# Two mixture-of-experts layers on one core: the first expert's products by halves around the gather, the last experts' sums around the up product, and the norm rows in the last down product

## Chip, core and metric

The kernel runs on one NeuronCore of a Trainium2 chip. The metric is the device time of one execution in microseconds (us), and the figure compared is the median of several executions. One execution was also recorded by the hardware profiler; its rows are what everything below is read from.

## What is computed

A trunk of two layers over 512 latent tokens (and 256 context tokens in layer 0) of width 1024. Each layer has a mixer (attention and pooling, then a short convolution) and after it a mixture of experts, which is where the change lies. Every one of 16 experts picks the 64 tokens with the highest affinity, so that the tokens of an expert are gathered, passed through three products with the expert's own weights, and summed back into the tokens' rows:

```python
def _expert_choice_ffn(u, w_router, w_g, w_u, w_d):
    b, n, _ = u.shape
    cap = CAPACITY_FACTOR * n // N_EXPERTS          # 64 of 512
    logits = jnp.einsum('bnd,de->ben', u, w_router, preferred_element_type=jnp.float32)
    aff = jax.nn.softmax(logits, axis=1)
    gate, idx = lax.top_k(aff, cap)
    bidx = jnp.arange(b)[:, None, None]
    xe = u[bidx, idx]
    hg = jnp.einsum('becd,edf->becf', xe, w_g)
    hu = jnp.einsum('becd,edf->becf', xe, w_u)
    ye = jnp.einsum('becf,efd->becd', jax.nn.silu(hg) * hu, w_d) * gate[..., None].astype(u.dtype)
    return jnp.zeros_like(u).at[bidx, idx].add(ye)

# in reference(), per layer:
h_lat = _post_norm(h_lat, m_lat[5] * f_lat, ln_ffn_g[layer], ln_ffn_b[layer])
```

Every weight of the three products is read once per execution: 16 experts x 3 matrices x 1024 x 1024 x 4 bytes are 201 MB in each layer, and 490 MB are moved in all.

## The kernel before

**Blocks and queue.** The weights pass through ten buffers of 2 MB, the blocks (names `blk`, numbered). Each of an expert's three matrices (`g`, `u`, `d`) is two blocks, one for each half of the contraction. `self.queue` lists all loads in the order in which they are used. A load is issued on the sync engine's queue (SP) at the point where a product has finished with a block: `next_load(b)` (L216 is its DMA) puts the next item of the queue into block `b` as one transfer of 2 MB; `next_half(b, h)` (L239) does the same in two transfers of 1 MB, the first as soon as half of the block has been read. With ten blocks, the block that a product frees is filled with weights used five products later. The last expert's `u` and `d` come in four pieces of 512 KB per block. SP issues in program order, so a transfer that waits for its block holds up those behind it.

**An expert.** `moe` runs over the experts in order. For expert `e`: `product("g", ...)` (16 rows of matmuls per half, L1341), `Silu` on ScalarE, `product("u", ...)`, `hid = silu(g) * u` on VectorE (L1401), four transposes of it (`p_t`, L1409) with a copy (`hT`, L1411), `scatter_sel` (one matmul `p_sb`, L1351, and a compare that gives the scatter matrix `st`), and `product("d", ...)`, whose result is scaled and split by `split_y`. The result of expert `e` is summed into the rows of all tokens during expert `e + 1`: `scatters(0)` and `scatters(2)`, four matmuls each (`p_sc`, L1369) and four VectorE updates (L1372). Up to expert 14 these stand behind the `u` product, on both sides of the transposes; in expert 15 they stand between the halves of `g` and behind `g`.

**The gather.** `gather` (L1319) forms the token columns `xe` of two experts, 16 matmuls for each half of the contraction, with ScalarE copies (L1328). For experts 2 to 15 it is spread over the preceding experts; for the first it runs where it is used: one half ahead of `g`, the other as `between`, ahead of the second half of `g`. Only the products `g` and `u` of expert 0 free their blocks by `next_half`; all others use `next_load`.

**The end of a layer.** The last `d` product is `out_mm`, in two column halves, with the sums (`sum_mm`, L1457) of the first half inside the second. In layer 1 the rows of the last norm's gain and shift (`ln_row`, 16 matmuls `p_gb`, L284, and four ScalarE copies) are made in expert 14, ahead of its `d` product, in a block that is no longer needed (`self.spare`). After it come the norm and the output. At three places in the kernel matmuls on zeros (`p_idle`) are run whose results nobody reads.

Of the kernel before, what the change touches and what calls it, by code (L numbers as in the profile page):

```python
# [16 lines left out]
P = 128  # L17
D = 1024
KO = D // P
# [6 lines left out]
KH = KO // 2  # L26
KEYS = S + C
KT = KEYS // P
NE = 16
# [96 lines left out]
def _pack(inp):  # L126
# [59 lines left out]
    rows=(4, 5, 9, 10, 15, 17),  # L186
# [4 lines left out]
class Trunk:  # L191
# [1094 lines left out]
    def moe(self, layer):  # L1286
        nc, tc, ins = self.nc, self.tc, self.ins
        last = layer == 1
# [4 lines left out]
        with tc.tile_pool(name=f"ex{layer}", bufs=2) as wk:  # L1293
            side = lambda v: [v[:, 0:512], v[:, 512:1024]]
            one = lambda name: wk.tile([P, 512], F32, name=name, bufs=1)
            g0 = side(wk.tile([P, D], F32, name="gb0", tag="yp", bufs=1)), [one("st"), one("hT")]
            rows = [lambda v=v: self.ln_row(4 * layer + v, g0[v], ALPHA) for v in range(2)]
# [14 lines left out]
            def gather(g, j0, j1, e0=0, e1=2, tag="sc"):  # L1312
                n = (e1 - e0) * CAP
                if j0 % KH == 0:
                    xes[g].append(wk.tile([P, KH, 2, CAP], F32, name="xe", bufs=3))
                pg = self.bank(tag, (P, j1 - j0, n), "p_ga")
                for j in range(j0, j1):
                    for t in range(TT):
                        nc.tensor.matmul(pg[:, j - j0], H[:, t, j * P:(j + 1) * P],  # L1319
                                         sels[g][:, t, e0:e1].rearrange("p e s -> p (e s)"),  # L1320
                                         start=t == 0, stop=t == TT - 1)
                for j in range(j0, j1):
                    o = xes[g][j // KH][:, j % KH, e0:e1].rearrange("p e s -> p (e s)")
                    if e1 - e0 == 1 and j % 2:
                        nc.vector.tensor_scalar(o, pg[:, j - j0], self.FG[:, 0, j:j + 1], self.FG[:, 1, j:j + 1],
                                                ALU.mult, ALU.add)
                    else:
                        nc.scalar.activation(o, pg[:, j - j0], AF.Identity, bias=self.FG[:, 1, j:j + 1],  # L1328
                                             scale=self.FG[:, 0, j:j + 1])

            def product(tag, lhs, name, between=None, by_halves=False):
                o = self.bank(tag)
                for h in range(2):
                    if h and between:
                        between()
                    W, b = self.w[f"{name}_{h}"]
                    W = W.rearrange("p (k n) -> p k n", k=KH)
                    for kk in range(KH):
                        k = h * KH + kk
                        for hf in range(2):  # L1340
                            nc.tensor.matmul(o[64 * hf:64 * hf + 64], lhs(k), W[:, kk, hf * 512:hf * 512 + 512],  # L1341
                                             start=k == 0, stop=k == KO - 1)
                        if by_halves and kk % 2:
                            self.next_half(b, kk // 2)
                    if not by_halves:
                        self.next_load(b)
                return o

            def scatter_sel(e):
                pb = self.bank("tr", name="p_sb")  # L1350
                nc.tensor.matmul(pb, self.identb[:, e:e + 1].to_broadcast([P, P]), self.slotb, start=True, stop=True)  # L1351
                st = wk.tile([P, S], F32R, name="st", bufs=1)
                nc.vector.tensor_scalar(st, pb, self.cv("slot1"), None, ALU.is_equal)
                return st

            def split_y(p_d, yp, m5):

                n = yp.shape[2]
                ye = self.rows()[:, 0:n]
                nc.vector.tensor_tensor(ye, p_d, m5, ALU.mult)  # L1360
                for hf in range(2):
                    r, q = slice(64 * hf, 64 * hf + 64), slice(64 - 64 * hf, 128 - 64 * hf)
                    nc.scalar.copy(yp[r, hf], ye[r])  # L1363
                    nc.vector.tensor_tensor(yp[q, hf], ye[r], yp[r, hf].bitcast(F32), ALU.subtract)  # L1364

            def scatter(e, st, yp, t):
                pp = [self.bank(name="p_sc") for _ in range(2)]
                for hf in range(2):
                    nc.tensor.matmul(pp[hf], st[:, t * P:(t + 1) * P], yp[:, hf], start=True, stop=True)  # L1369
                for hf in range(2):  # L1370
                    a = A[:, t, hf * 512:hf * 512 + 512]
                    nc.vector.scalar_tensor_tensor(a, pp[hf], self.gateT[:, t, e:e + 1], a, ALU.mult, ALU.add)  # L1372
# [4 lines left out]
            for t in range(TT):  # L1377
                self.residual(t, g0)
            gather(0, 0, 4)
            prev, gb = None, []  # L1380
            for e in range(NE):
                xe = xes[e // 2]
                before = prev

                def scatters(t0):
                    for t in (t0, t0 + 1) if before else ():
                        scatter(*before, t)

                p_g = product("g", lambda k: xe[k // KH][:, k % KH, e % 2], f"g{layer}_{e}", (lambda: scatters(0) if e == NE - 1 else None) if e else lambda: gather(0, 4, KO), e == 0)
                sg = wk.tile([P, 512], F32, name="sg", bufs=1)  # L1390
                nc.scalar.activation(sg, p_g, AF.Silu)  # L1391
                if e == NE - 1:
                    scatters(2)
                g = e // 2 + 1
                if g < NE // 2 and e % 2 == 0:
                    sel_build(g)
                p_u = product("u", lambda k: xe[k // KH][:, k % KH, e % 2], f"u{layer}_{e}", None, e == 0)
                if e == 0 and self.late:
                    self.late()
                hid = self.rows()  # L1400
                nc.vector.tensor_tensor(hid, sg, p_u, ALU.mult)  # L1401

                if e < NE - 1:
                    scatters(0)
                if g < NE // 2:
                    gather(g, 4 * (e % 2), 4 * (e % 2) + 4, tag="g")
                p_t = self.bank("tr", (P, 4, P), "p_t")
                for q in range(4):
                    nc.tensor.transpose(p_t[:, q], hid[:, q * P:(q + 1) * P], self.cv("ident"))  # L1409
                hT = wk.tile([P, 4, P], F32, name="hT", bufs=1)  # L1410
                nc.vector.tensor_copy(hT, p_t)  # L1411
                if e < NE - 1:
                    scatters(2)
                st = scatter_sel(e)
                if last and self.spare and not gb:
                    gb += [self.spare[:, v * D:v * D + D] for v in range(2)]
                    g1 = [side(v) for v in gb]
                    for v in range(2):
                        self.ln_row(4 * layer + 2 + v, g1[v], 1.0)
                lhs = lambda k: hT[:, k % 4, (k // 4) * CAP:(k // 4) * CAP + CAP]  # L1420
                yp = wk.tile([P, 2, 512], F32R, name="yp", bufs=1)
                if e < NE - 1:
                    split_y(product("d", lhs, f"d{layer}_{e}"), yp, self.m5b)
                    prev = (e, st, yp)
            nc.scalar.preload_act_table_set("natural_log_exp_and_others")

# [9 lines left out]
            def out_mm(c, k0, k1):  # L1436
                W, b = self.w[f"d{layer}_{e}_{c}"]
                W = W.rearrange("p (k n) -> p k n", k=KO)
                for k in range(k0, k1):
                    for q in range(2):  # L1440
                        nc.tensor.matmul(outs[c][64 * q:64 * q + 64], lhs(k), W[:, k, q * 256:q * 256 + 256],
                                         start=k == 0, stop=k == KO - 1)
                if k1 == KO:
                    self.next_load(b)
                    split_y(outs[c], yps[:, c], m5[:, c])
# [21 lines left out]
            hs = wk.tile([P, TT, 2], F32, name="l_hs", bufs=1)  # L1467
# [34 lines left out]
                return self.rsqrt(x, v, wk)  # L1502

            out_mm(0, 0, KO)
            out_mm(1, 0, KH)
            for t in range(TT):
                if t < 2 + last:
# [8 lines left out]
            if last:  # L1516
# [42 lines left out]
                idle = self.bank(name="p_idle")  # L1559
# [196 lines left out]
```

## Time and profile before

| | |
|---|---|
| median of 3 runs | 1444.56 us (1442.07 to 1447.09) |
| the profiled execution | 1447.51 us |
| its span, first to last instruction | 1445.7 us |
| TensorE (PE) busy | 1379.2 us, 95% |
| VectorE (DVE), ScalarE (ACT), GpSimd (POOL) busy | 48%, 23%, 8% |
| moved by DMA | 490.35 MB, 339 GB/s over the span |
| mean granted TensorE clock | 0.979 |

The page cuts the span into 40 slices of 36 us. The experts of layer 0 run from about 291 to 740 us and those of layer 1 from about 971 to 1422 us; in both stretches the DMA row reads 9 in nearly every slice, at 426 or 427 GB/s, and so does the PE row. Busy PE is not PE at its peak, since ends of matmuls are modelled. PEclk is the clock granted to TensorE: 1.00 is 2.4 GHz and 0.50 is 1.2 GHz.

### The profile page before, as it was taken

The numbers are of one execution on the slowest core, as the hardware profiler recorded it, in microseconds if no ns is written. First come the engines' busy times: TensorE is split into PE (matmuls) and PEld (weight loads), VectorE is DVE, ScalarE is ACT, GpSimd is POOL, SyncE is SP. The second block draws the span as 40 slices with busy tenths as digits, with TensorE's granted clock in tenths as the row PEclk, the third lists the DMA queues.
The fourth block names the chain that finished last, engine by engine and source line by source line (L and its number), as shares of the span: only waits on it lengthen the run. The fifth ranks groups of instructions, "written<-read, shape, count | busy, mean of one in ns | idle before, by whom it ended". The sixth has DMA issues, their size and how long they took to land.

```text
span 1445.7 us, 17480 instructions
## 1 busy us (share of the span) xinstructions
PE 1379.2 (95%) x7212; PEld 766.8 (53%) x7212; DVE 690.1 (48%) x1221; ACT 333.7 (23%) x654; POOL 120.1 (8%) x151
## 2 busy tenths in 40 slices
PE   7999989899999999999979999999999999999996
PEld 4875547654444444444358787764444444444333
DVE  3574758713343343333466878761343343343245
ACT  3455661311011011011143223141111111111112
POOL 3111630050000000000020000014000000000000
PEclk9999999899999999999989999999999999999998
DMA  9347337989999999999974554659999999999991
GB/s 369 140 162 302 128 123 305 380 305 420 427 426 427 427 427 425 427 427 426 418 289 150 221 226 190 251 243 374 428 426 426 427 427 427 426 426 427 426 404 62
DMA packets 42527, 490.35 MB, mean 339 GB/s; under 512 B 4752, under 2 KB 5200, under 8 KB 13136
## 3 DMA queue, kind: packets, MB, share of 16 engines
q1 hardware_dynamic: 41856, 486.10, 81.5%
q10 hardware_dynamic: 592, 3.15, 0.6%
q8 instruction: 56, 0.92, 0.3%
q14 instruction: 23, 0.19, 0.0%
HBM read 487.13 MB, written 2.10 MB: 338 GB/s over the span
## 4 chain that ended last, share of the span: by engine, by line
PE 65%; DMA 20%; DVE 10%; ACT 2%; issue 1%; POOL 0%; DVEq 0%; SPq 0%; ACTq 0%
PE p_g L1341 11%; PE p_d L1341 10%; PE p_u L1341 10%; DMA blk<-wu 7%; DMA blk<-wg 5%; DMA blk<-wd 5%; PE p_ga_g L1319 5%; PE p_sc_sc L1369 3%; DMA blk<-wmod 2%; PE p_c_sc L253 2%; PE p_c_sc L255 2%; PE p_c_sc L254 2%; PE p_y_sc L253 2%; PE p_y_sc L255 2%; PE p_y_sc L254 1%; PE p_o L947 1%
## 5 line engine op out<-in xcount | busy, mean ns | idle before, releaser
L1341 PE MATMUL p_u<-blk,xe 128*64 128x512 f32 x1024 | 226.3, 593 | 6.3 <-DMA blk<-wu 6.3
L1341 PE MATMUL p_g<-blk,xe 128*64 128x512 f32 x1024 | 226.4, 593 | 2.3 <-ACT xe L1328 2.2
L1341 PE MATMUL p_d<-blk,hT 128*64 128x512 f32 x960 | 214.9, 601 | 0.0
L1401 DVE TENSOR_TENSOR rows<-sg,p_u 128x512 f32<-128x512 f32 x32 | 22.0, 688 | 325.6 <-PE p_u L1341 315.5
L1341 PEld LDWEIGHTS p_u<-blk,xe 128*64 128x64 f32 x1024 | 72.5, 137 | 154.5 <-issue 139.7
L1341 PEld LDWEIGHTS p_g<-blk,xe 128*64 128x64 f32 x1024 | 72.6, 137 | 147.2 <-issue 139.7
L1341 PEld LDWEIGHTS p_d<-blk,hT 128*64 128x64 f32 x960 | 66.5, 138 | 131.0 <-issue 130.9
L1328 ACT ACTIVATE xe<-p_ga_g,FG 128x128 f32<-128x128 f32 x112 | 42.1, 456 | 306.8 <-PE p_ga_g L1319 306.8
L1363 ACT CAST yp<-rows 64x512 fp32r<-64x512 f32 (+1 forms) x68 | 40.2, 591 | 283.6 <-DVE rows L1360 282.8
L1360 DVE TENSOR_TENSOR rows<-p_d,m5b 128x512 f32<-128x512 f32 x30 | 20.8, 692 | 136.1 <-PE p_d L1341 136.1
L1372 DVE SCALAR_TENSOR_TENSOR A<-p_sc_sc,gates,A 128x512 f32<-128x512 f32 x120 | 81.6, 743 | 3.0 <-PE p_sc_sc L1369 3.0
L1372 DVE SCALAR_TENSOR_TENSOR H<-p_sc_sc,gates,H 128x512 f32<-128x512 f32 x120 | 81.6, 743 | 3.0 <-PE p_sc_sc L1369 3.0
L1369 PE MATMUL p_sc_sc<-yp,st 128*128 128x512 f32 x240 | 72.9, 421 | 0.9 <-DVE H L1372 0.5
L253 PE MATMUL p_c_sc<-blk,blk 128*128 128x512 f32 x168 | 66.9, 398 | 0.0
L255 PE MATMUL p_c_sc<-blk,blk 128*128 128x512 f32 x168 | 65.5, 390 | 0.0
L254 PE MATMUL p_c_sc<-blk,blk 128*128 128x512 f32 x168 | 65.4, 390 | 0.0
L1431 POOL COPY m5c<-m5b 64x256 f32<-64x256 f32 x8 | 3.2, 394 | 718.0 <-PE p_ga_g L1319 717.6
L1369 PEld LDWEIGHTS p_sc_sc<-yp,st 128*128 128x128 f32 x240 | 40.7, 189 | 34.3 <-issue 24.3
L1364 DVE TENSOR_TENSOR yp<-rows,yp 64x512 fp32r<-64x512 f32 (+1 forms) x68 | 44.6, 655 | 25.3 <-ACT yp L1363 24.2
L1391 ACT ACTIVATE sg<-p_g 128x512 f32<-128x512 f32 x32 | 19.1, 597 | 155.0 <-PE p_g L1341 155.0
L1319 PEld LDWEIGHTS p_ga_g<-sel,A 128*128 128x128 f32 x448 | 52.1, 192 | 1.9 <-issue 0.8
L1319 PEld LDWEIGHTS p_ga_g<-sel,H 128*128 128x128 f32 x448 | 52.1, 192 | 1.1
(424 smaller groups left out, 2043.1 us busy)
## 6 DMA issues: line engine op xcount, KB each, us to landing
blk<-wg SPq DMA_DIRECT2D x60, 2048.0 KB, 28.1
blk<-wu SPq DMA_DIRECT2D x60, 2048.0 KB, 22.2
blk<-wd SPq DMA_DIRECT2D x56, 2048.0 KB, 26.4
blk<-wmod SPq DMA_DIRECT2D x23, 2048.0 KB, 9.9
blk<-wci SPq DMA_DIRECT2D x8, 1536.0 KB, 11.6
blk<-wd SPq DMA_DIRECT2D x8, 1024.0 KB, 7.4
blk<-wg SPq DMA_DIRECT2D x8, 1024.0 KB, 9.4
blk<-wu SPq DMA_DIRECT2D x16, 512.0 KB, 22.9
```

The lines of the kernel that those rows point to most:

```text
L253: mm(out, ah, bh, start=start, stop=False)
L254: mm(out, ah, bl, start=False, stop=False)
L255: mm(out, al, bh, start=False, stop=stop)
L1319: nc.tensor.matmul(pg[:, j - j0], H[:, t, j * P:(j + 1) * P], sels[g][:, t, e0:e1].rearrange("p e s -> p (e s)"), start=t == 0, stop=t == ...
L1328: nc.scalar.activation(o, pg[:, j - j0], AF.Identity, bias=self.FG[:, 1, j:j + 1], scale=self.FG[:, 0, j:j + 1])
L1341: nc.tensor.matmul(o[64 * hf:64 * hf + 64], lhs(k), W[:, kk, hf * 512:hf * 512 + 512], start=k == 0, stop=k == KO - 1)
L1360: nc.vector.tensor_tensor(ye, p_d, m5, ALU.mult)
L1363: nc.scalar.copy(yp[r, hf], ye[r])
L1364: nc.vector.tensor_tensor(yp[q, hf], ye[r], yp[r, hf].bitcast(F32), ALU.subtract)
L1369: nc.tensor.matmul(pp[hf], st[:, t * P:(t + 1) * P], yp[:, hf], start=True, stop=True)
L1372: nc.vector.scalar_tensor_tensor(a, pp[hf], self.gateT[:, t, e:e + 1], a, ALU.mult, ALU.add)
L1401: nc.vector.tensor_tensor(hid, sg, p_u, ALU.mult)
```

## The change

Five things are different.

1. In expert 0 the first halves of `g` and of `u` run one behind the other ahead of the second gather, and the second halves behind it. Each frees its block by `next_half`.
2. Expert 0's `d` and all products of expert 1 free their blocks by `next_half` too (`e < 2`).
3. In expert 14 `scatters(0)` moves ahead of the `u` product, `scatters(2)` between its halves.
4. In experts 14 and 15 three matmuls on zeros stand behind `u` and three behind the transposes.
5. In layer 1 `ln_row` moves from expert 14 into the last `d` product, behind its first column half.

```diff
-            def product(tag, lhs, name, between=None, by_halves=False):
-                o = self.bank(tag)
-                for h in range(2):
+            def product(tag, lhs, name, between=None, by_halves=False, hs=(0, 1), o=None):
+                if o is None:
+                    o = self.bank(tag)
+                for h in hs:
                     if h and between:
                         between()
...
-                p_g = product("g", lambda k: xe[k // KH][:, k % KH, e % 2], f"g{layer}_{e}", (lambda: scatters(0) if e == NE - 1 else None) if e else lambda: gather(0, 4, KO), e == 0)
+                rows = lambda k: xe[k // KH][:, k % KH, e % 2]
+                p_u = None
+                if e == 0:
+
+                    p_g, p_u = (product(q, rows, f"{q}{layer}_0", None, True, (0,)) for q in "gu")
+                    gather(0, 4, KO)
+                    product("g", rows, f"g{layer}_0", None, True, (1,), p_g)
+                else:
+                    p_g = product("g", rows, f"g{layer}_{e}", lambda: scatters(0) if e == NE - 1 else None, e < 2)
...
-                p_u = product("u", lambda k: xe[k // KH][:, k % KH, e % 2], f"u{layer}_{e}", None, e == 0)
+
+                if e == NE - 2:
+                    scatters(0)
+                p_u = product("u", rows, f"u{layer}_{e}",
+                              (lambda: scatters(2)) if e == NE - 2 else None, e < 2, (0, 1) if e else (1,), p_u)
+                if e > NE - 3:
+                    idle = self.bank(name="p_idle")
+                    for _ in range(3):
+                        nc.tensor.matmul(idle, self.slotb[:, 0:P], self.slotb, start=True, stop=True)
...
-                if e < NE - 1:
+                if e < NE - 2:
                     scatters(0)
...
-                if e < NE - 1:
+                if e < NE - 2:
                     scatters(2)
+                else:
+                    for _ in range(3):
+                        nc.tensor.matmul(idle, self.slotb[:, 0:P], self.slotb, start=True, stop=True)
                 st = scatter_sel(e)
-                if last and self.spare and not gb:
-                    gb += [self.spare[:, v * D:v * D + D] for v in range(2)]
-                    g1 = [side(v) for v in gb]
-                    for v in range(2):
-                        self.ln_row(4 * layer + 2 + v, g1[v], 1.0)
...
-                    split_y(product("d", lhs, f"d{layer}_{e}"), yp, self.m5b)
+                    split_y(product("d", lhs, f"d{layer}_{e}", None, e < 2), yp, self.m5b)
...
             out_mm(0, 0, KO)
+            if last:
+                gb = [self.spare[:, v * D:v * D + D] for v in range(2)]
+                for v in range(2):
+                    self.ln_row(4 * layer + 2 + v, side(gb[v]), 1.0)
             out_mm(1, 0, KH)
```

How the instructions stand now. On SP, in expert 0 and 1 of layer 0 (`blk_38` and `blk_39` hold expert 0's `d`, `blk_40` to `blk_43` expert 1's `g` and `u`). Before:

```order
L239 DMA blk_34_1838<-wd 128x2048 x2
L239 DMA blk_35_1895<-wd 128x2048 x2
L239 DMA blk_36_1897<-wg 128x2048 x2
L239 DMA blk_37_1899<-wg 128x2048 x2
L216 DMA blk_44_2516<-wu 128x4096
L216 DMA blk_45_2526<-wu 128x4096
L216 DMA blk_46_2543<-wd 128x4096
```

After, the same place on SP:

```order
L239 DMA blk_34_1838<-wd 128x2048 x2
L239 DMA blk_36_1897<-wd 128x2048 x2
L239 DMA blk_35_1895<-wg 128x2048 x2
L239 DMA blk_37_1899<-wg 128x2048 x2
L239 DMA blk_38_2004<-wu 128x2048 x2
L239 DMA blk_39_2071<-wu 128x2048 x2
L239 DMA blk_40_2194<-wd 128x2048 x2
```

The second and third blocks to be refilled have changed places, and the loads behind the four first ones, single transfers of 2 MB before, are pairs of 1 MB.

On PE, in expert 14 of layer 1, from the second half of `g` to the `d` product (`p_sc` are the sums of expert 13, `p_gb` the norm rows). Before:

```order
L1341 MATMUL p_g<-blk_233_7948,xe 64x512 x8
L1341 MATMUL p_u<-blk_234_8019,xe 64x512 x8
L1341 MATMUL p_u<-blk_235_8029,xe 64x512 x8
L1369 MATMUL p_sc_sc<-yp,st 128x512 x4
L1409 MATMUL p_t_tr<-cst,rows 128x128 x4
L1369 MATMUL p_sc_sc<-yp,st 128x512 x4
L1351 LDWEIGHTS identb
L1351 MATMUL p_sb_tr<-slotb,identb 128x512
L284 MATMUL p_gb_sc<-lnr,pick 128x128 x16
L1341 MATMUL p_d<-blk_236_8046,hT 64x512 x8
```

After, from the same half of `g` to the first of the matmuls on zeros:

```order
L1342 MATMUL p_g<-blk_217_7962,xe 64x512 x8
L1370 MATMUL p_sc_sc<-yp,st 128x512 x4
L1342 MATMUL p_u<-blk_218_8033,xe 64x512 x8
L1370 MATMUL p_sc_sc<-yp,st 128x512 x4
L1342 MATMUL p_u<-blk_219_8043,xe 64x512 x8
L1414 LDWEIGHTS slotb
L1414 MATMUL p_idle_sc<-slotb 128x512
```

The eight sums stand ahead of the two halves of `u`, the matmuls on zeros stand where they were, and the norm rows are gone from here.

On PE, in the last `d` product of layer 1 (`out_mm`; `p_d` is its first column half, `p_u` its second, `p_sc` the sums of the first). Before:

```order
L1441 MATMUL p_d<-blk_242_8183,hT 64x256 x16
L1441 MATMUL p_u<-blk_243_8196,hT 64x256 x8
L1457 MATMUL p_sc_sc<-yp,st 128x256 x8
L1441 MATMUL p_u<-blk_243_8196,hT 64x256 x8
L1525 MATMUL p_z_g<-lnr,pick 128x128 x4
```

After, the same place:

```order
L1456 MATMUL p_d<-blk_226_8197,hT 64x256 x16
L284 MATMUL p_gb_sc<-lnr,pick 128x128 x16
L1456 MATMUL p_u<-blk_227_8210,hT 64x256 x8
L1472 MATMUL p_sc_sc<-yp,st 128x256 x8
L1456 MATMUL p_u<-blk_227_8210,hT 64x256 x8
L1544 MATMUL p_z_g<-lnr,pick 128x128 x4
```

The norm rows now stand between the two column halves.

## Rows read from the trace of the kernel before

**Rows 1.** Busy time by stretch: us from:to, length, engines, PEclk, DMA share, GB/s.
```profile
400.00:700.00 300.00, 296.33 (x1523) 131.80 (x1522) 106.77 (x160) 36.25 (x77) 1.57 (x4) 1.00 1.01 427
```

**Rows 2.** Timeline of PE, end of layer 0: start us, length, what [idle before].
```profile
663.31 3.65 PE L1341 MATMUL p_u<-blk,xe 128*64 128x512 f32 x16 [1.25 <-DMA blk<-wu]
...
687.83 3.65 PE L1341 MATMUL p_u<-blk,xe 128*64 128x512 f32 x16 [0.70 <-DMA blk<-wu]
692.74 3.65 PE L1341 MATMUL p_u<-blk,xe 128*64 128x512 f32 x16 [1.26 <-DMA blk<-wu]
696.32 1.20 PE L1369 MATMUL p_sc_sc<-yp,st 128*128 128x512 f32 x4
...
700.78 7.09 PE L1341 MATMUL p_d<-blk,hT 128*64 128x512 f32 x32
...
712.38 3.65 PE L1341 MATMUL p_g<-blk,xe 128*64 128x512 f32 x16
...
717.11 7.09 PE L1341 MATMUL p_u<-blk,xe 128*64 128x512 f32 x32
725.04 0.66 PE L1409 MATMUL p_t_tr<-cst,rows 128*128 128x128 f32 x4 [0.85 <-DVE rows L1401]
726.48 0.38 PE L1351 MATMUL p_sb_tr<-slotb,identb 128*128 128x512 bf16 x1 [0.78 <-DVE hT L1411]
726.79 3.67 PE L1441 MATMUL p_d<-blk,hT 128*64 128x256 f32 x32
```

**Rows 3.** Timeline of PE, end of layer 1.
```profile
1371.70 3.65 PE L1341 MATMUL p_u<-blk,xe 128*64 128x512 f32 x16 [1.25 <-DMA blk<-wu]
...
1380.10 3.28 PE L284 MATMUL p_gb_sc<-lnr,pick 128*128 128x128 f32 x16 [0.28 <-DVE H L1372]
1383.31 9.34 PE L1341 MATMUL p_d<-blk,hT 128*64 128x512 f32 x32
...
1401.85 7.09 PE L1341 MATMUL p_u<-blk,xe 128*64 128x512 f32 x32
...
1411.53 5.36 PE L1441 MATMUL p_d<-blk,hT 128*64 128x256 f32 x32
...
1419.89 1.95 PE L1441 MATMUL p_u<-blk,hT 128*64 128x256 f32 x16
```

**Rows 4.** Busy time by stretch, as rows 1, inside the `d` product of expert 14.
```profile
1384.00:1386.00 2.00, 2.00 (x8) 0.55 (x6) 0.00 (x0) 0.01 (x1) 0.00 (x0) 0.50 1.02 434
```

**Rows 5.** Timeline of SP, first transfers of experts 0 and 1 in both layers.
```profile
305.15 0.33 SPq L239 DMA_DIRECT2D blk<-wd  x1
306.86 0.33 SPq L239 DMA_DIRECT2D blk<-wd  x1
...
312.01 2.04 SPq L239 DMA_DIRECT2D blk<-wg  x2
...
323.64 3.76 SPq L216 DMA_DIRECT2D blk<-wu  x2
...
1002.47 3.76 SPq L216 DMA_DIRECT2D blk<-wu  x2
```

**Rows 6.** Issue to landing (us, last) of those at 305.15, 306.86, 312.01, 313.73, 323.64.
```profile
blk<-wd SPq DMA_DIRECT2D x1, 1024.0 KB, 5.4
blk<-wd SPq DMA_DIRECT2D x1, 1024.0 KB, 6.8
...
blk<-wg SPq DMA_DIRECT2D x1, 1024.0 KB, 9.1
blk<-wg SPq DMA_DIRECT2D x1, 1024.0 KB, 9.8
...
blk<-wu SPq DMA_DIRECT2D x1, 2048.0 KB, 8.2
```

**Rows 7.** Timeline of PE, start of layer 0's experts.
```profile
279.45 1.98 PE L284 MATMUL p_gb_sc<-lnr,pick 128*128 128x128 f32 x16
...
319.94 7.09 PE L1341 MATMUL p_d<-blk,hT 128*64 128x512 f32 x32
```

More of the change, by code (lines that the diff above doesn't have):

```diff
@@ L1379, in moe @@
             gather(0, 0, 4)
-            prev, gb = None, []
+            prev = None
             for e in range(NE):
```

## The prediction

> **What bounds the kernel now.** I read first the busy time by stretch. Inside an expert layer both the DMA engines and TensorE (PE) are full: from 400 to 700 us DMA is busy at 1.01 and 427 GB/s, PE for 296.33 of 300 us at full clock [rows 1]. Which of the two is last can't be told from shares, so I went to the timeline of PE at the end of each layer. There it is DMA. PE waits 1.25 us for expert 13's second `u` block, 0.70 and 1.26 us for expert 14's two [rows 2]; layer 1 shows the same, with 1.25 us in front of expert 14's second half [rows 3]. The two starts that waited, 687.83 and 692.74, are 4.91 us apart: that is the time of a 2 MB block at 427 GB/s (2.097 / 0.427), so blocks land at the full rate and PE takes them as they come. All experts before that run without such waits; PE uses up the stock of ten blocks and meets the DMA only here. So what is gained in an expert layer is bounded by how much earlier its transfers run, not by how many instructions PE has.
>
> Where did DMA lose time? At the layer's start, seen on SP's timeline and in the time from issue to landing. The last transfer set free by the first `g` and `u` is issued at 313.73 and takes 9.8 us, so it lands at 323.5; the next is not issued before 323.64 [rows 5, 6], when expert 0's `d` product, begun at 319.94 [rows 7], has read a whole block. It is alone in the queue and lands 8.2 us later [rows 6], against 4.91 for a block behind others.
>
> The end of layer 1 has a second loss. The `d` product of expert 14 takes 9.34 us there and 7.09 in layer 0; the first half of the last `d` 5.36 against 3.67 [rows 2, 3]. The granted clock explains it: inside the first it is 0.50, the 1.2 GHz level [rows 4], after a stretch in which PE waited 1.25 us for DMA and then, ahead of the norm rows, for VectorE [rows 3].
>
> **The change part by part.** *Halves around the gather (expert 0).* PE does the same work in another order: it costs nothing. `u`'s first block comes free one gather earlier, so SP issues the second pair of transfers that much sooner. But everything that expert 0's `g` and `u` set free has landed at 323.5 already, ahead of the next issue. In layer 0 this part moves DMA's idle time from ahead of that issue to an earlier place, gain 0. In layer 1 it only keeps the queue from being in the way of the next part.
>
> *`d` of expert 0 and all of expert 1 by halves.* The first transfer behind the pause needs half a block read, not a whole one. A block takes 3.43 us (the two issues behind 323.64 end 3.76 us later, the last lasting 0.33 [rows 5]), so the issue is 1.72 us sooner. The first 1 MB lands 5.4 us after its issue when it meets an empty queue, the second 2.45 behind it, 7.85 together against 8.2 [rows 6]: 0.35 more. Lead of all later transfers: 2.05 us, in layer 1 the same, where the issue stands at 1002.47 [rows 5]. Bounds: 1.7 (the issue alone) and 2.4 (had the second half come at once). Pieces of 1 MB behind each other land at the full rate: 312.01 + 9.1 and 313.73 + 9.8 are 2.42 us apart [rows 5, 6]. The transfers behind are saturated as before, so the lead holds to the layer's end.
>
> *Sums of expert 13 around `u` of expert 14, with the end of layer 0 walked through.* Four sums take PE about 1.05 us (1.20 with the overlap [rows 2]). The waits before were 1.25 + 0.70 up to `u`'s first half, so without them PE would be there at 687.83 - 1.95 = 685.9. Sums: 686.9; the block, due at 687.83 - 2.05 = 685.8, is there. First half 3.43: 690.4. Sums: 691.4; the second block is due at 692.74 - 2.05 = 690.7. Second half: 694.8. From the end of `u` to `d` I take expert 15 as it is, where the sums don't stand there either: 717.11 + 6.87 to 726.79 are 2.81 us [rows 2]. `d` at 697.6 instead of 700.78. Then DMA is last again: `g` of expert 15 has its first block three blocks behind the second of `u`, 692.74 + 14.7 - 2.05 = 705.4, while PE is there at 697.6 + 6.9 = 704.5: a new wait of 0.9. A half and its sums take some 4.6, so the second block, due at 710.3, is waited for again, 0.3; from there a half and sums are 4.73 as before (712.38 to 717.11), and `u` begins at 715.0 [rows 2]. So 3.2 us stand at `d` and 2.1 at `u`: layer 0 ends **2.1 us** sooner, DMA's lead and no more. The moved sums by themselves fill waits that the lead has removed.
>
> *Matmuls on zeros.* The three behind `u` and three behind the transposes stand where PE idles 0.85 and 0.78 us. `p_sb`, of the same shape in bf16, has the next product 0.31 behind its start [rows 2], start-up included, so three take at most 0.93. I count 0: in a row they should be shorter than one alone. If not, it is up to 0.15 at each of eight places, 1.0 in all; at half the clock (three times 0.62 against the same pauses) about 1 us at a place, 4 in layer 1.
>
> *End of layer 1.* The same walk: `u`'s second half at 1371.70 - 2.05 = 1369.65, done at 1373.1, `d` at 1375.9 instead of 1383.31; of these 7.4 us 3.5 are the norm rows and their wait, now gone from here. If the clock stays up, `d` takes 6.9: 1382.8. `g`'s first block lands at 1371.70 + 14.7 - 2.05 = 1384.35, a wait of 1.5; the second at 1389.3, a wait of 0.4; 4.73 behind it `u` at 1394.0 instead of 1401.85 [rows 3], 7.8 us. The last `d` follows 9.68 us behind, as before, and its first half takes 3.67, not 5.36: 1.7 us more. The norm rows come next. At full clock they take 1.98 us, about 1.85 on the path [rows 7]; I count them in full, since PE had other work there before too: 1.85 back. ScalarE's four copies must clear the banks for the sums that follow; the next quarter of the product, 1.8, covers them; else they cost up to 2, the whole of the rows again. The last quarter comes 7.8 + 1.7 - 1.85 = 7.65 us sooner than at 1419.89, and the norm and output behind it are unchanged: layer 1 ends **7.7 us** sooner.
>
> *Sum.* 2.1 + 7.7 = 9.8 us off the profiled execution's 1447.51: 1437.7. That execution is 3 us above the median of the runs shown, 1444.56. It may simply be a slower one (then 1434.8), or the half-clock stretches, 2.25 + 1.7 us, are in it and not in every run (then those runs gain less, and the sum stays). The lowest run, 1442.07, is 5.4 below it, which suits the second, so I take 1437, nearer to the upper end.
>
> The Trainium skill's page "TensorE: Matmul & The Clock Gate", section "Part 1: The HAM clock gate", says that the clock is low by default, that activity releases it, and that the moment varies from run to run. The trace agrees in that layer 0 kept its clock through waits like those that layer 1 lost it after.
>
> **The rivals.** *The clock falls all the same.* PE still has the new waits of 1.5 and 0.4 us ahead of expert 15's halves. If it runs at half clock for as long as before, the 2.25 and 1.7 us come back: 1441.6. Against it: the two waits for DMA of expert 14 and that for VectorE are gone, and the pauses of 0.85 and 0.78 are filled.
>
> *The lead doesn't come.* If the halves only move the idle time, blocks land when they do now. Then the sums still fill waits in expert 14, but DMA takes it back at expert 15: layer 0 gains about 0.1, layer 1 about 5.7 (7.7 less 2.05; norm rows and clock are left): 1441.7. For it speaks only that landing times of pieces vary by some tenths.
>
> *Fillers and copies in the way.* Zeros 1.0 and the banks of the norm rows up to 2: 1440.7 with both in full.
>
> *Halves are dearer (slower than before).* The first two pieces behind a pause, 305.15 + 5.4 and 306.86 + 6.8, land 3.1 us apart, not 2.42 [rows 5, 6]: 0.69 us lost on a piece. Sixteen more pieces a layer at that price are 11 us, and both layers' ends are DMA's: 1437.7 + 22 = 1460. It decides for slower from (9.8 + 4.3) / 32 = 0.44 us a piece. Against it: pieces that queue, as all but the first would, show no loss. The Trainium skill, "DMA: Bandwidth & Descriptors", section "Bandwidth", puts a 1 MB transfer at 341 GB/s and 16 MB at 425; by that a piece of 1 MB would lose about 0.6 us (an estimate from that page), which is this rival. The rows of queued pieces disagree with it.
>
> **How the numbers follow.** Forecast 1437: 0.72. Clock 0.11, no lead 0.06, fillers 0.08, dearer halves 0.03. About 0.3% (4.3 us) is what a measurement of this kernel tells from no change, so faster means under 1440.2: the forecast and half of the fillers' and part of the clock's case, 0.81; same 0.15; slower 0.04. The range goes from 1432.5 (the lower base, 1434.8, less 0.7 for a lead of 2.4 in both layers, less 1.6, since the runs shown spread 2.5 about their median) to 1441.5 (nearly up to either of the two at 1441.6).
>
> **What would show it.** In the changed profile: the first 1 MB behind the pause issued some 1.7 us after PE begins expert 0's `d`; no wait ahead of expert 13's `u` and none over 0.3 ahead of 14's; a wait of about 1 to 1.5 ahead of `g` of expert 15; 6.2 us from the second half of expert 14's `u` to its `d`; granted clock 1.00 through both `d` products of layer 1's last experts; norm rows of about 1.98 us behind the first half of the last `d`. I am wrong if the waits for DMA stay at their size (no lead), if pieces of 1 MB land over 2.5 us apart, or if the clock reads 0.50 in those products.

## The result and the profile after

The changed kernel takes **1437.01 us** (median of 5 runs, 1436.18 to 1439.6), the kernel before beside it 1444.56 (5 runs, 1441.14 to 1448.56): ratio 0.9948, 95% interval 0.9929 to 0.9967. The prediction said 1437. The profiled execution took 1437.01 us, and its span is 1435.2; before, these were 1447.51 and 1445.7.

The first view is the timeline of PE at the end of layer 0 in the changed kernel (start us, length, what, idle time before it); it answers to [rows 2].

```profile
660.35 3.65 PE L1342 MATMUL p_u<-blk,xe 128*64 128x512 f32 x16 [0.83 <-DMA blk<-wu]
...
685.26 3.65 PE L1342 MATMUL p_u<-blk,xe 128*64 128x512 f32 x16
688.84 1.21 PE L1370 MATMUL p_sc_sc<-yp,st 128*128 128x512 f32 x4
689.98 3.65 PE L1342 MATMUL p_u<-blk,xe 128*64 128x512 f32 x16
693.57 0.82 PE L1414 MATMUL p_idle_sc<-slotb 128*128 128x512 bf16 x3
694.48 0.66 PE L1426 MATMUL p_t_tr<-cst,rows 128*128 128x128 f32 x4
694.98 0.81 PE L1433 MATMUL p_idle_sc<-slotb 128*128 128x512 bf16 x3
...
696.23 7.09 PE L1342 MATMUL p_d<-blk,hT 128*64 128x512 f32 x32
704.56 3.65 PE L1342 MATMUL p_g<-blk,xe 128*64 128x512 f32 x16 [1.25 <-DMA blk<-wg]
...
709.40 3.65 PE L1342 MATMUL p_g<-blk,xe 128*64 128x512 f32 x16
...
714.11 7.09 PE L1342 MATMUL p_u<-blk,xe 128*64 128x512 f32 x32
...
723.79 3.67 PE L1456 MATMUL p_d<-blk,hT 128*64 128x256 f32 x32
```

The waits ahead of expert 14's `u` are gone, the sums stand in their place, and a new wait of 1.25 us stands ahead of expert 15's `g`: DMA is last again, as the walk through the layer said. The wait ahead of expert 13's `u`, which the prediction expected to be gone, has shrunk from 1.25 to 0.83 only.

The same view at the end of layer 1, against [rows 3]:

```profile
1366.35 3.65 PE L1342 MATMUL p_u<-blk,xe 128*64 128x512 f32 x16
1369.93 0.82 PE L1414 MATMUL p_idle_sc<-slotb 128*128 128x512 bf16 x3
...
1372.59 7.22 PE L1342 MATMUL p_d<-blk,hT 128*64 128x512 f32 x32
1381.15 3.65 PE L1342 MATMUL p_g<-blk,xe 128*64 128x512 f32 x16 [1.34 <-DMA blk<-wg]
...
1390.73 7.09 PE L1342 MATMUL p_u<-blk,xe 128*64 128x512 f32 x32
...
1400.40 3.67 PE L1456 MATMUL p_d<-blk,hT 128*64 128x256 f32 x32
1404.01 2.00 PE L284 MATMUL p_gb_sc<-lnr,pick 128*128 128x128 f32 x16
1405.94 1.95 PE L1456 MATMUL p_u<-blk,hT 128*64 128x256 f32 x16
1407.82 1.21 PE L1472 MATMUL p_sc_sc<-yp,st 128*128 128x256 f32 x8
1408.96 1.95 PE L1456 MATMUL p_u<-blk,hT 128*64 128x256 f32 x16
```

The two down products take 7.22 and 3.67 us, not 9.34 and 5.36. The clock in them, and the middle of layer 0, by stretch (columns as [rows 1]; the clock is the third number from the end). The stretch at 1384 is that of [rows 4], but PE is in expert 15's `g` by then; expert 14's `d` lies in the last one:

```profile
400.00:700.00 300.00, 298.94 (x1539) 132.73 (x1537) 108.50 (x162) 35.19 (x73) 1.57 (x4) 1.00 1.01 427
1384.00:1386.00 2.00, 1.93 (x8) 0.67 (x4) 0.73 (x2) 0.00 (x0) 0.00 (x0) 1.00 0.96 387
1372.00:1380.00 8.00, 7.68 (x34) 2.12 (x32) 1.12 (x3) 0.00 (x0) 0.00 (x0) 1.00 1.01 430
```

At a layer's start the timeline of PE, against [rows 7]:

```profile
288.47 3.81 PE L1319 MATMUL p_ga_sc<-sel,H 128*128 128x128 f32 x32
...
317.58 7.09 PE L1342 MATMUL p_d<-blk,hT 128*64 128x512 f32 x32
```

and the issue on SP's timeline of the four pieces of 1 MB behind the pause, against [rows 5]:

```profile
319.55 5.48 SPq L239 DMA_DIRECT2D blk<-wu  x4
```

The time from issue to landing (us, last) of the first three of them, issued at 319.55, 321.27 and 322.99, against [rows 6]:

```profile
blk<-wu SPq DMA_DIRECT2D x1, 1024.0 KB, 5.1
...
blk<-wu SPq DMA_DIRECT2D x1, 1024.0 KB, 6.9
...
blk<-wu SPq DMA_DIRECT2D x1, 1024.0 KB, 7.6
```

The first piece is issued 1.97 us behind the start of `d`, against 3.70 before (323.64 - 319.94). They land at 324.65, 328.17 and 330.59: 3.5 us apart, then 2.4. Over 2.5 us was one of the prediction's signs of being wrong, and between the first two it has come.

To compare executions that start a little apart, I measure each stage from the layer's first gather (its first `p_ga` on PE). Profiled executions, us:

| kernel | up to layer 0's first gather | to the last `d` of layer 0 | to layer 1's gather | to the last quarter of its last `d` | rest | span |
|---|---|---|---|---|---|---|
| before | 290.84 | 435.95 | 243.77 | 449.33 | 25.81 | 1445.7 |
| after | 288.47 | 435.32 | 241.82 | 443.35 | 26.24 | 1435.2 |
| difference | -2.37 | -0.63 | -1.95 | -5.98 | +0.43 | -10.5 |

Only the second and fourth columns hold what was changed: 6.6 us. The other 3.9 are no work of the change. In this execution of before the clock was below full at 210 to 230 us (0.86 and 0.97) and at 900 to 910 (0.84); in the changed one it was 1.00 there. The 6.6 hang on the execution of before, too: against its second profile (further down: 436.48 and 446.20 us in the two columns) the changed stages are 1.16 and 2.85 us shorter, 4.0 in all.

### The profile page after: what moved, and what is told of

Its sections match the earlier page's. It is cut to its first block, busy times and chain, and to the rows that moved or that the text cites. A ratio compares the mean times of both kernels' runs of the same rounds, so it can differ in the third digit from the quotient of the medians.

```text
span 1435.2 us, 17562 instructions
## 1 busy us (share of the span) xinstructions
PE 1374.9 (96%) x7236; PEld 763.8 (53%) x7236; DVE 688.9 (48%) x1221; ACT 333.5 (23%) x654; POOL 120.1 (8%) x151
## 4 chain that ended last, share of the span: by engine, by line
PE 68%; DMA 17%; DVE 10%; ACT 3%; issue 2%; POOL 0%; SPq 0%; DVEq 0%; ACTq 0%; POOLq 0%
PE p_g L1342 11%; PE p_u L1342 11%; PE p_d L1342 11%; DMA blk<-wd 6%; PE p_ga_g L1319 5%; DMA blk<-wg 5%; DMA blk<-wu 5%; PE p_sc_sc L1370 3%; PE p_y_sc L253 2%; PE p_y_sc L255 2%; PE p_y_sc L254 2%; PE p_c_sc L253 2%; PE p_c_sc L255 2%; PE p_c_sc L254 2%; DVE rows L358 2%
```

## The experiments

The changed parts are numbered as in the section on the change. All runs below went beside runs of the kernel before, in three groups; kernels of different groups are compared by their ratios. "Zeros" is short for the idle matmuls of part 4, whose result nobody reads. Their operand `slotb` is not all zeros: it is set to zero once, and then `nc.scalar.copy(self.slotb[:NE], pr)` (L1280) writes the experts' slot numbers into 16 of its 128 rows.

**Halves alone** (before, with parts 1 and 2):

```diff
+                p_u = product("u", rows, f"u{layer}_{e}", None, e < 2, (0, 1) if e else (1,), p_u)
...
+                    split_y(product("d", lhs, f"d{layer}_{e}", None, e < 2), yp, self.m5b)
```

> The kernel before with the first two parts of the change alone: expert 0's halves around the gather, and blocks freed by halves in experts 0 and 1. As the prediction has it, transfers lead by 2.05 us in each layer and the waits ahead of the last up products shrink by that: 4.1 us faster than before, about 1440.5. By the trace of the changed kernel, in which the second half of expert 14's up product starts 401.5 us after the layer's first gather and before 401.9 (layer 1: 400.7 and 401.1), the lead is 0.5 us: 1 us faster, about 1443.5. In both cases expert 14 of layer 1 still has the norm rows ahead of its down product.

Measured 1443.43 us (12 runs, 1438.34 to 1447.97) against 1444.74 (24 runs), ratio 0.9987 (0.9972 to 1.0002). By the median the halves bring 1.3 us, beside the 1 us of the second expectation; two times 2.05 is just beyond the interval's end (4.0 us). In layer 1 the clock fell in expert 14's `d` as in before, but not in the last `d` (3.67 us); PE there:

```profile
1377.19 2.43 PE L284 MATMUL p_gb_sc<-lnr,pick 128*128 128x128 f32 x16 [0.28 <-DVE H L1373]
1379.54 8.79 PE L1342 MATMUL p_d<-blk,hT 128*64 128x512 f32 x32
```

**All but the halves** (after, with parts 1 and 2 undone):

```diff
...
-                    split_y(product("d", lhs, f"d{layer}_{e}", None, e < 2), yp, self.m5b)
+                    split_y(product("d", lhs, f"d{layer}_{e}"), yp, self.m5b)
```

> The changed kernel with the first two parts undone: old order in expert 0, blocks freed whole from expert 0's down product on. The prediction's lead of 2.05 us in each layer would be lost: 4 us above the changed kernel, about 1441. By a lead of 0.5 us: 1 us above it, about 1438.

1439.3 us (7 runs), ratio 0.9956 (0.994 to 0.9972): nearly the whole gain is left, and the time is nearer to the 1438 of a small lead than to the 1441 of the predicted one.

**All but the zeros** (after, without part 4):

```diff
-                if e > NE - 3:
-                    idle = self.bank(name="p_idle")
-                    for _ in range(3):
-                        nc.tensor.matmul(idle, self.slotb[:, 0:P], self.slotb, start=True, stop=True)
```

and the three behind the transposes likewise.

> The changed kernel without the twelve matmuls on zeros in each layer's experts 14 and 15. If these keep the clock up, the granted clock falls to 0.50 again in a down product of layer 1, at 1.7 to 2.3 us each: 1439 to 1441. If pauses of 0.9 us are too short to matter and what cost the clock were the waits for transfers and the norm rows: no difference, 1437 within 1.

1442.39 us (12 runs), ratio 0.998 (0.9968 to 0.9992): about half of the gain is lost, where the prediction had 0 for this part, and more than the 1439 to 1441 expected. PE's timeline at the end of layer 1 in this kernel shows why:

```profile
1374.22 0.66 PE L1422 MATMUL p_t_tr<-cst,rows 128*128 128x128 f32 x4 [0.85 <-DVE rows L1414]
1375.66 0.38 PE L1352 MATMUL p_sb_tr<-slotb,identb 128*128 128x512 bf16 x1 [0.78 <-DVE hT L1424]
1375.96 8.78 PE L1342 MATMUL p_d<-blk,hT 128*64 128x512 f32 x32
...
1403.66 5.36 PE L1449 MATMUL p_d<-blk,hT 128*64 128x256 f32 x32
```

with the clock by stretch inside the two products:

```profile
1376.00:1380.00 4.00, 4.00 (x13) 1.25 (x14) 0.75 (x1) 0.00 (x0) 0.00 (x0) 0.57 1.00 426
1404.00:1408.00 4.00, 4.00 (x26) 2.37 (x24) 0.52 (x1) 0.00 (x0) 0.00 (x0) 0.60 0.55 220
```

No wait for DMA stands ahead of expert 14's `u` here, and the norm rows are out of the way; only the pauses of 0.85 and 0.78 us are back, and the clock falls in both products. The kernel differs from the changed one in the zeros alone, and there the products take 7.22 and 3.67 us: the zeros are not idle cover, they hold the clock in this place.

**Norm rows back in expert 14** (after, without part 5):

```diff
                 st = scatter_sel(e)
+                if last and self.spare and not gb:
...
-            if last:
-                gb = [self.spare[:, v * D:v * D + D] for v in range(2)]
...
```

> The changed kernel with the norm rows back in expert 14, ahead of its down product. If they belong where the change has them, as the prediction counts it: their 2 us return ahead of the down product, with them a wait for VectorE and perhaps the clock: 1438 to 1441. The rival: in the changed kernel PE waits 1.34 us for a transfer right behind that down product, which would cover most of the 2 us, and the last down product is shorter by 1.93: 1 to 1.9 us faster than the changed kernel, about 1435.5.

1437.1 us (6 runs), ratio 0.9939 (0.9922 to 0.9956): no slower than the changed kernel, and in the profile 2.8 us shorter in layer 1 (440.54 from the gather to the last quarter). Neither of the two expected times came; it lies between them. PE's timeline of it:

```profile
1375.38 2.08 PE L284 MATMUL p_gb_sc<-lnr,pick 128*128 128x128 f32 x16
1377.40 7.09 PE L1342 MATMUL p_d<-blk,hT 128*64 128x512 f32 x32
1384.32 3.60 PE L1342 MATMUL p_g<-blk,xe 128*64 128x512 f32 x16
...
1403.38 3.67 PE L1461 MATMUL p_d<-blk,hT 128*64 128x256 f32 x32
...
1410.05 1.95 PE L1461 MATMUL p_u<-blk,hT 128*64 128x256 f32 x16
```

Ahead of expert 15's `g` there is no wait now: the rows stand where PE would otherwise wait 1.34 us for DMA. From the last `d` to the last quarter it is 6.67 us here and 8.56 in the changed kernel. Two more pairs of kernels that differ in this alone say the same: all but the halves against sums and zeros (below) 443.77 and 441.87, and the last two kernels below 442.08 and 439.93. Not all of this is part 5, since some of it lies ahead of expert 14's `d`. From the start of that `d`, or of the norm rows where they stand ahead of it, to the last quarter it is 34.67 us in each of the three kernels with the rows in expert 14, and 36.37, 36.36 and 36.71 in their partners. So part 5 costs 1.7 to 2.0 us of layer 1 in the profiles; the times don't tell the kernels of a pair apart.

**The changed kernel again**, beside the next kernels (no edit).

> The changed kernel once more, beside the three below. Theory: its gain is that of layer 1's end (no fall of the clock in the two last down products, 3.9 us, and about 2 us of waits), so its granted clock should read 1.00 there again and its median lie within 1 us of 1437. If the first result owed much to luck elsewhere (the execution of before that was profiled shows two half-clock stretches outside the changed stretches, the one of the changed kernel none), it is 1438 to 1439.

1438.04 us (6 runs, 1435.82 to 1440.66) against 1443.16 (11 runs), ratio 0.9963 (0.9948 to 0.9978); span of the profile 1434.0. The median is 1.0 us above the first one, at the border of the two cases expected. The clock held again: the two products take 7.09 and 3.67 us.

**Sums and zeros alone** (before, with parts 3 and 4):

```diff
+                if e == NE - 2:
+                    scatters(0)
+                p_u = product("u", rows, f"u{layer}_{e}",
+                              (lambda: scatters(2)) if e == NE - 2 else None, e == 0)
+                if e > NE - 3:
+                    idle = self.bank(name="p_idle")
...
```

> The kernel before with the sums around the up product and the matmuls on zeros alone: no halves beyond those of before, norm rows where they were. Theory: these two are the core of the gain; the halves add some 1.4 us (no_halves was 2.3 above the changed kernel, halves_only 1.3 below before), the norm rows' move nothing: 1438 to 1439. If the parts only work together: above 1441.

1438.49 us (6 runs), ratio 0.9965 (0.9952 to 0.9979): these two parts are the change, as far as times can tell. The clock holds, with the norm rows ahead of `d` as in before (PE):

```profile
1376.92 7.09 PE L1342 MATMUL p_d<-blk,hT 128*64 128x512 f32 x32
...
1402.89 3.67 PE L1454 MATMUL p_d<-blk,hT 128*64 128x256 f32 x32
```

**Sums alone** (before, with part 3):

```diff
+                if e == NE - 2:
+                    scatters(0)
...
-                if e < NE - 1:
+                if e < NE - 2:
                     scatters(0)
```

> The kernel before with one part alone: the sums of expert 13 stand around expert 14's up product; no matmuls on zeros, no halves, norm rows in their old place. Theory now: TensorE keeps full clock in layer 1's last two down products only where the pauses of 0.85 and 0.78 us ahead of them are filled. Then this kernel loses the clock in at least one of them and comes out 3 to 5 us above the kernel with sums and zeros (1438.5), at 1442 to 1444. Rival: the sums' move alone keeps the clock, since it takes away the waits for DMA in expert 14; then 1438 to 1440, and the zeros are worth nothing without the other parts.

Half right. The profile is as the theory said, the clock falls in both products on PE's timeline:

```profile
1372.55 0.66 PE L1411 MATMUL p_t_tr<-cst,rows 128*128 128x128 f32 x4 [0.85 <-DVE rows L1403]
...
1377.06 9.34 PE L1341 MATMUL p_d<-blk,hT 128*64 128x512 f32 x32
...
1405.29 5.36 PE L1443 MATMUL p_d<-blk,hT 128*64 128x256 f32 x32
```

But the median is 1440.1 us (12 runs against 1445.11), ratio 0.9972 (0.9953 to 0.9991), below the 1442 to 1444 expected and not to be told from sums with zeros. Its runs spread widely, from 1434.33 to 1446.83. So zeros are worth 2.5 to 4.6 us in the full change (0.998 against 0.9963 and 0.9948) and about 1 us with the sums alone; between these their price stays open. (All but the zeros has parts 1, 2 and 5 as well, which sums alone has not; some of what lies between these two, 0.998 against 0.9972, may be part 5.)

**Old order in expert 0** (after, with part 1 alone undone):

```diff
-                    p_g, p_u = (product(q, rows, f"{q}{layer}_0", None, True, (0,)) for q in "gu")
-                    gather(0, 4, KO)
-                    product("g", rows, f"g{layer}_0", None, True, (1,), p_g)
...
+                p_g = product("g", rows, f"g{layer}_{e}", (lambda: scatters(0) if e == NE - 1 else None) if e else lambda: gather(0, 4, KO), e < 2)
...
```

> The changed kernel with its first part undone: expert 0's gate product whole around the gather, as before, all the halves of transfers kept. The prediction gave that part nothing in layer 0 and in layer 1 no more than a queue out of the way. By it this run is within 1 us of the changed kernel (1437 to 1438.5). Rival: the order around the gather is what brings the 1 us that both first parts gave together; then it is 1 us or more above it (1438.5 to 1440).

1438.72 us (12 runs), ratio 0.9966 (0.9951 to 0.998). By microseconds it lies 0.2 past the line of 1438.5, by the ratio beside the changed kernel's 0.9963: no effect that can be measured. Its stages agree with that: 435.31 us in layer 0 and 443.86 in layer 1 (changed kernel 435.32 and 443.35).

**The kernel before, profiled again** (no edit).

> The kernel before, profiled a second time. If its half-clock stretches in the down products of layer 1's experts 14 and 15 belong to the kernel, they are there again: 8.5 to 9.4 us for expert 14's and 5.4 for the first half of expert 15's. If they were chance like those at 210 to 230 and 890 to 910 us, some of them are gone (7.1 and 3.7), and stretches stand elsewhere; time 1442 to 1449 either way.

1443.82 us (1 run). Of the half-clock stretches one is there again and one is not, though the pauses of 0.85 and 0.78 us stand ahead of the last `d` as before. PE's timeline:

```profile
1380.25 8.37 PE L1341 MATMUL p_d<-blk,hT 128*64 128x512 f32 x32
...
1407.19 0.38 PE L1351 MATMUL p_sb_tr<-slotb,identb 128*128 128x512 bf16 x1 [0.78 <-DVE hT L1411]
1407.50 3.67 PE L1441 MATMUL p_d<-blk,hT 128*64 128x256 f32 x32
```

At 210 to 230 and 890 to 910 us the clock is 1.00 this time.

**The gather spread out.** In the changed kernel expert 0's `d` waits behind the gather for the next two experts. Here a quarter of that gather stays, a quarter goes behind the transposes and a half behind `d`:

```diff
-                if g < NE // 2:
+                if e == 0:
+                    gather(1, 0, 1)
+                elif g < NE // 2:
                     gather(g, 4 * (e % 2), 4 * (e % 2) + 4, tag="g")
...
+                if e == 0:
+                    gather(1, 1, 2)
...
+                    if e == 0:
+                        gather(1, 2, 4)
```

> The changed kernel with expert 0's share of the next gather spread: a quarter behind its up product, a quarter behind the transposes, half behind its down product. Then PE reaches that down product some 1.9 us sooner, frees its first block sooner and doesn't idle the 0.85 us behind the transposes. If what a layer takes is set by how early transfers restart behind the pause: 1 to 2 us off each layer, 1433 to 1435. If other starts bind (the pause is followed by pieces that land 3.5 us apart): under 0.5 us a layer, 1436 to 1437.

1436.0 us (5 runs), ratio 0.995 (0.9935 to 0.9964). PE's timeline shows the earlier `d` and what it costs:

```profile
287.91 3.81 PE L1319 MATMUL p_ga_sc<-sel,H 128*128 128x128 f32 x32
...
315.10 7.09 PE L1342 MATMUL p_d<-blk,hT 128*64 128x512 f32 x32
322.11 2.05 PE L1319 MATMUL p_ga_sc<-sel,H 128*128 128x128 f32 x16
324.09 7.09 PE L1342 MATMUL p_g<-blk,xe 128*64 128x512 f32 x32
```

`d` begins 27.2 us behind the first gather instead of 29.1; layer 0 takes 434.4, layer 1 442.08. The time is at the lower edge of the second case expected (1436 to 1437). Layer 0 is 0.4 to 0.9 us shorter and layer 1 1.1 to 1.3, against the two profiles of the changed kernel, for a `d` that starts 1.9 us sooner in layer 0.

**Both of these together** (gather spread, norm rows back in expert 14):

> The changed kernel with the norm rows back in expert 14 and the gather spread as in gather_spread. Norm rows: the stretch from layer 1's first gather to the last quarter of its last product was 440.5 us with them back and 443.4 in the changed kernel, so 1 to 2.8 us. With the gather's 0 to 4: 1431 to 1436. If the clock falls in expert 14 behind the norm rows as it did before: 1438 to 1439.

**1434.03 us** (6 runs, 1428.13 to 1436.64), ratio 0.993 (0.9911 to 0.9949): 4.0 us below the changed kernel beside it by the medians, 9.1 below the kernel before, and inside the 1431 to 1436 expected. The edits are those of the two kernels above.

## Where the prediction was right and where not

**Total: right, by luck; two errors met.** The sum was 9.8 us; the changed stages gave 6.6, and 4.0 against the second profile of before. It was taken off an execution that lay 2.95 us above its median, and its surplus was only partly what the prediction took it for: 3.9 us of the two profiles' difference lie where nothing was changed. From the median, 1444.56 - 6.6 would be 1438.0. By the medians the two sets of runs gave 7.6 and 5.1 us (1444.56 - 1437.01, 1443.16 - 1438.04).

**The lead of DMA, 2.05 us a layer: mis-sized.** It lies outside both bounds given for it, 1.7 and 2.4, and how 2.4 follows is not shown. The step's first half held in layer 0: the issue comes 1.73 us sooner after `d` (1.72 predicted). Then the second piece lands 8.62 us behind the first one's issue (328.17 - 319.55), not 7.85; with the halves alone it is 8.61 and with the old order 9.02. I had given the second piece the 2.4 us of queued ones, though a pair at 3.1 stood in [rows 5, 6], which I kept for a rival. From the layer's first gather, this block lands 1.3 us sooner than before (39.70 against 331.84 - 290.84 = 41.00), and the start of expert 13's second `u` half, which waits for DMA in both, is 0.6 us sooner (371.88 against 372.47). Most of the 0.7 between goes while the pieces of 1 MB flow, which the prediction had at the rate of whole blocks. In 30 us behind the first of them, at full DMA share, before moves 427 GB/s and the changed kernel 420 (columns as [rows 1]):

```profile
332.84:362.84 30.00, 30.00 (x157) 13.33 (x155) 10.07 (x15) 3.93 (x8) 0.00 (x0) 1.00 1.00 427
330.47:360.47 30.00, 30.00 (x157) 13.31 (x155) 10.06 (x15) 3.93 (x8) 0.00 (x0) 1.00 1.01 420
```

The same stretch reads 420 to 422 in both layers of six profiles with parts 1 and 2, or part 2 alone, and 427 to 429 in both layers of five without them; further on, from 80 to 360 us behind the gather, all eleven read 426 or 427. That is some 0.5 us a layer (an estimate: 30 us times 7 in 427).

In layer 1 the step failed earlier. The issue is 1.7 us sooner there too (995.80 - 965.61 = 30.19 behind the gather, before 1002.47 - 970.56 = 31.91), but the block lands only 0.2 sooner (997.52 + 8.0 - 965.61 = 39.91, before 1002.47 + 8.2 - 970.56 = 40.11). The prediction took layer 0's pause for layer 1 as well. In layer 0 of before the last earlier piece landed at 323.5, ahead of the issue at 323.64; in layer 1 it was issued at 993.45 and landed 11.3 us later:

```profile
blk<-wg SPq DMA_DIRECT2D x1, 1024.0 KB, 11.3
```

That is 1004.75, 2.3 us behind the issue at 1002.47, so an earlier issue had less of a pause to shorten. That this is the reason is argued, not tested.

The miss of 1.5 us a layer is nearly the whole miss of the sum: at `u` of expert 15 the walk said 2.1 us for layer 0, and 0.63 came (425.64 from the gather against 426.27); it said 7.65 for layer 1's last quarter, and 5.98 came. Over all profiles layer 0 takes 435.42 us with the halves of the transfers in their places (mean of 6, the spread gather left out) and 436.16 without (mean of 5); single profiles of the two groups overlap (436.09 with, 435.93 without).

**Halves around the gather, 0: right**, as far as the old order's time and stages show. `d` stands 29.11 us behind the first gather, before 29.10.

**The sums' move and the walk: right in shape.** Wait ahead of expert 15's `g` 1.25 (0.9 predicted) and 1.34 (1.5 predicted); 6.25 us from the second half of `u` to `d` (6.2).

**Zeros, cost 0: right, but the step missed what they do.** From the end of `u` to the last `d` it is 2.81 us as before, and three zeros take 0.82. I counted them as harmless cover and blamed the low clock on the waits for DMA and VectorE. The runs say otherwise: without zeros the clock falls in expert 14's `d` of layer 1 even where those waits are gone (all but the zeros, sums alone), and with zeros it stays at 1.00 behind a wait for DMA of 1.34 us ahead of expert 15's `g`. By the product's length in every profile:

| kernels | `d` of expert 14, layer 1 | first half of the last `d` |
|---|---|---|
| no zeros: before, before again, halves, all but zeros, sums | 9.34, 8.37, 8.79, 8.78, 9.34 | 5.36, 3.67, 3.67, 5.36, 5.36 |
| zeros (8 profiles) | 7.09 to 7.22 | 3.67 in each |

The Trainium skill, "TensorE: Matmul & The Clock Gate", section "A second HAM failure mode: psum-queue depth-cycling", says that short idle times between groups of matmuls, if frequent, make the clock swing between its levels. The two kernels with the pauses of 0.85 and 0.78 us ahead of expert 14's `d` in layer 1 agree with it. Not settled is when such pauses cost the clock. In the five profiles without zeros the pair of pauses stands at seven places of layer 1 (ahead of the last `d` in all, ahead of expert 14's in two), and the clock fell behind five of them; of the same seven places in layer 0 it fell behind none. In the other three of the five, what stands ahead of expert 14's `d` in layer 1 are waits for DMA of 0.7 to 1.3 us and for VectorE of 0.15 to 0.28.

**The clock in the run times.** The mean granted clock goes with the time of a run also within one kernel: among the 58 runs of before that went beside these kernels, the means are 1447.07 us at 0.979 (8 runs), 1444.34 at 0.981 (20), 1441.96 at 0.983 (7), 1439.24 at 0.985 (2): 1.3 us for 0.001. The changed kernel's second set has 1437.99 us at 0.9843 by the means, before beside it 1443.59 at 0.9817: some 3.4 of the 5.6 us between go with the clock. This is a relation, not an experiment; that zeros raise the clock rests on the kernels with and without them.

**Norm rows, 1.85 back at the end: right, but the move was a loss.** The prediction's own walk had a wait of 1.5 and 0.4 us take over 1.9 of the 3.5 us that the rows left in expert 14, and it did not draw the conclusion. At full clock the rows cost 2.0 us there (1375.38 to 1377.40), and the wait for DMA covers 1.3; at the end nothing covers their 1.9. The copies that clear the banks cost nothing more (the next quarter begins 1.93 us after the rows' start, and the sums follow it without a pause).

**Rivals.** Dearer halves: at a small part of that rival's price; most pieces behind each other land 2.4 to 2.5 us apart, and 420 against 427 GB/s is 0.04 us on a piece (an estimate), not 0.69. No lead: nearly so, some 0.6 of the 2.05 us came in layer 0, and 0.2 at the landing of that block in layer 1. Clock falls all the same: not here, but it does as soon as the zeros are gone.

## What to carry to other kernels

When a trace shows a low clock, look at the short pauses ahead of it as well as at the long waits, and try filling them: here a few matmuls whose result nobody reads held the clock that the reordering alone lost. A pause of the queue that one layer shows is to be looked for in the other layer too before a lead is counted there. A step moved off a path is a gain only if the next wait there doesn't swallow it and the new place covers it: put it where the engine waits for DMA anyway. Before a sum is made against one profiled execution, compare the clock of the stretches that the change doesn't touch.

## What the hardware did that was not expected

- Two pauses under 1 us (0.85 and 0.78), in a PE that is otherwise full, went with a fall to the lower clock at five of seven places in layer 1 and at none of seven in layer 0; with three matmuls of 128 by 512 in each pause (0.82 us) the clock fell at none of 16 places of layer 1 in eight profiles. Zeros filled 112 of the 128 rows of their operand.
- In layer 0, after a gap of 8 us in the queue's issues, 1 MB landed 5.1 us after its issue (5.9 with the halves alone, 6.5 with the old order), and the second, issued 1.72 us later, 8.6 to 9.0 us after the first one's issue; from then on most landed 2.4 to 2.5 us apart.
- Pieces of 1 MB kept the DMA share at 1.00 or 1.01 but moved 420 to 422 GB/s over 30 us, where blocks of 2 MB moved 427 to 429.
- The mean clock of one kernel differs by 0.007 from run to run (before: 0.978 to 0.985), and its time by 13 us (1438.31 to 1451.48).
